# Hybrid encoder layer on one core: the input projection with fp16 high and low parts in place of rounded fp32 parts

## The chip, the cores and the metric

The kernel runs on one core of one Trainium2 chip. The core has five engines with queues of their own: TensorE (PE, matmuls, with its weight loads shown apart as PEld), VectorE (DVE), ScalarE (ACT), GpSimd (POOL) and SyncE (SP, which here only issues DMAs). Each engine works through its queue in order and waits on semaphores of the others. The metric is the device time of one execution in microseconds; lower is better.

## The reference, cut to what matters

One layer of an encoder over x of 2048 tokens and 1024 columns: a norm and an input projection, attention in three dilated windows beside a convolution branch, an output projection, cross-attention to a memory of 256 rows, an MLP, and a last norm. The change is in the first line:

```python
y = rmsnorm(h, norm_mix_g[l]) @ w_in[l]                 # 2048 x 1024 @ 1024 x 2560
q = partial_rotary(y[..., 0:D_ATT]...)                  # 512 columns
k = partial_rotary(y[..., D_ATT:2 * D_ATT]...)          # 512 columns
v = y[..., 2 * D_ATT:3 * D_ATT]...                      # 512 columns
conv = conformer_conv(a, g, ...)                        # 512 columns each; a * sigmoid(g) first
```

All inputs and outputs are float32.

## The kernel before

**Two parts for each operand.** A matmul operand is held as a high part (the value rounded to fp32r, a rounded fp32 format that TensorE reads) and a low part (what the rounding left). `mm3` (L198) makes three matmuls of a product: high by high, high by low, low by high. `wsplit2` (L187) makes the pair of a weight tile of 128 x 1024: ACT copies `raw` to `hi` (L190), DVE or POOL subtracts to `lo` (L191).

**Layout.** x stands transposed: 8 chunks of 128 columns (k) by 4 token groups of 512 (n). `xprep` (L322) loads the natural rows of one group (`xn`), gets the norm's factors per token from squares on ACT (L310), turns each chunk on TensorE (`xt`, L334), stores it for the residual (`xscr`), multiplies by the norm's gain and factor on DVE (`xv`, L339) and splits: ACT to `xh` (L340), POOL to `xl` (L341). A weight tile is 128 output columns of w_in; with 512 tokens it takes 8 x 3 = 24 matmuls (`linear_steps`, into `lin`), moving 512 columns each.

**The units.** `glu` (L507) makes two units for each 128 columns of the convolution branch: g (through a tanh on ACT) and a (times the gate on DVE, stored to `uscr`). `lin_qk` (L606) makes a q or k unit over all four groups; c = "r" gathers the 16 rotary columns of each of the 8 heads with eight DMAs of small pieces, c = 0, 1, 2 the other 48. `lin_v` (L561) makes v with tokens as output rows and 256 columns moving, from weights that were scaled by a power of two per column block (`vscale`, L534: squares of the weights on ACT, a column sum on TensorE, a power on POOL, a bit mask and a reciprocal on DVE). `pinned` and `after` only tell the scheduler that an instruction is to be placed behind another one.

**The order.** `pipeline` (L494) runs the units one after another and keeps two ahead: when unit i starts, the weights of i + 1 are split and the load of i + 2 is issued. A unit's first step issues the DMA of `raw`, its second splits. `raw`, `whi` and `wlo` have two buffers each, so the load of unit i + 2 waits until the low part of unit i is made; the zero row of `edges` (L726) takes a turn in the `raw` buffers between the rotary q tile and the first k tile. All loads stand in SP's queue in a fixed order, so a load that waits holds up those behind it. The units run in this order: g and a of column chunks 0 and 1 for groups 0 and 1; k and q rotary; k and q 0, 1, 2; g and a of chunk 2, v of the first 256 columns, g and a of chunk 3, v of the others; and then, woven into the attention of the first 512 queries, g and a of all four chunks for groups 2 and 3 (`rest`). The projections of the memory for cross-attention (`memory`, L348; their last products are `pb`, evacuated by ACT to `eb`, L464) and the first two groups of x come ahead of all this; groups 2 and 3 of x are prepared while the first units run. The convolution (`conv_unit`, L213, on DVE) runs beside the q, k and v units. The order of each engine's instructions is made by a scheduler from the program's order and its own model of time when the program is built.

## Time and profile before

| | |
|---|---|
| runs, us | 2844.74, 2839.31, 2848.41 |
| median, us | 2844.74 |
| span of the profiled execution, us | 2842.4 |
| DMA | 434.27 MB, mean 153 GB/s |
| projection units ahead of attention | 136.6 to about 524 us (with start and end of `lin` and `v`) |
| late units, woven into attention | about 524 to 713 us |

The profile is of one execution of its own, whose span is the time from its first instruction to its last. Busy times of an engine count its instructions' durations; matmuls are pipelined, so a duration (389 ns for a matmul of 512 columns) is longer than the distance from one start to the next, and it is the latter that says how fast TensorE goes. "Chain" is the work that ended last, followed back from the end. Names are those of the program's tiles: `whi_u<-raw_u` writes `whi_u` from `raw_u`. A row of a group gives its line, engine, operation, names, shape and count, its busy time, and the mean duration in ns. In the timeline the first number is the start from the span's beginning and the second the duration; "[1.69 <-POOL vs L554]" says that the engine was idle for 1.69 us before it, until that instruction ended.

### The profile page before, as it was taken

The numbers are of one execution on the slowest core, as the hardware profiler recorded it, in microseconds if no ns is written. First come the engines' busy times: TensorE is split into PE (matmuls) and PEld (weight loads), VectorE is DVE, ScalarE is ACT, GpSimd is POOL, SyncE is SP. The second block draws the span as 40 slices with busy tenths as digits, with TensorE's granted clock in tenths as the row PEclk, the third lists the DMA queues.
The fourth block names the chain that finished last, engine by engine and source line by source line (L and its number), as shares of the span: only waits on it lengthen the run. The fifth ranks groups of instructions, "written<-read, shape, count | busy, mean of one in ns | idle before, by whom it ended". The sixth has DMA issues, their size and how long they took to land.

```text
span 2842.4 us, 41222 instructions
## 1 busy us (share of the span) xinstructions
PE 2795.1 (98%) x15440; PEld 2355.0 (83%) x15440; DVE 1961.5 (69%) x3473; ACT 1203.8 (42%) x2055; POOL 466.6 (16%) x483
## 2 busy tenths in 40 slices
PE   8999999999999999999999999999999999999998
PEld 7888899888788888888888888888888888888887
DVE  6636536465789786557887755589886646569886
ACT  6633211475554333434443344444433434444443
POOL 1336421122102012200021012001110210000000
PEclk9999999999999999999999999999999999999999
DMA  8979855799734444554444535534444445223332
GB/s 267 304 168 233 203 137 137 182 259 261 201 102 134 128 138 130 166 150 158 122 126 129 149 111 181 176 112 134 130 133 129 142 152 178 90 89 98 92 115 67
DMA packets 590729, 434.27 MB, mean 153 GB/s; under 512 B 191581, under 2 KB 508433, under 8 KB 590016
## 3 DMA queue, kind: packets, MB, share of 16 engines
q1 hardware_dynamic: 549776, 407.68, 50.1%
q10 hardware_dynamic: 38528, 17.93, 2.5%
q0 software_dynamic: 2224, 6.01, 0.6%
q8 instruction: 122, 2.00, 0.3%
q14 instruction: 79, 0.65, 0.1%
HBM read 340.42 MB, written 91.11 MB: 152 GB/s over the span
## 4 chain that ended last, share of the span: by engine, by line
PE 86%; DVE 7%; DMA 3%; issue 1%; ACT 1%; POOL 0%; SPq 0%; DVEq 0%; POOLq 0%; ACTq 0%
PE dn L200 8%; PE dn L201 8%; PE dn L202 8%; PE up L200 7%; PE up L202 7%; PE up L201 7%; PE lin L200 4%; PE lin L202 4%; PE lin L201 4%; PE pt L795 2%; PE o L200 2%; PE o L202 2%; PE o L201 2%; PE xs L200 2%; PE xs L202 2%; PE xs L201 2%
## 5 line engine op out<-in xcount | busy, mean ns | idle before, releaser
L200 PE MATMUL up<-mh,whi_u 128*128 128x512 f32 x1024 | 403.4, 394 | 0.0
L201 PE MATMUL up<-ml,whi_u 128*128 128x512 f32 x1024 | 399.6, 390 | 1.9 <-DVE ml L1239 1.9
L202 PE MATMUL up<-mh,wlo_u 128*128 128x512 f32 x1024 | 399.2, 390 | 0.0
L217 DVE SCALAR_TENSOR_TENSOR cacc<-cu,cw,cacc 128x512 f32<-128x512 f32 x480 | 387.1, 807 | 5.4
L200 PE MATMUL dn<-hhh,whi_d 128*128 128x512 f32 x768 | 299.1, 399 | 1.1 <-ACT hhh L1350 1.1
L201 PE MATMUL dn<-hhl,whi_d 128*128 128x512 f32 x768 | 298.7, 391 | 0.6 <-DVE hhl L1351 0.6
L202 PE MATMUL dn<-hhh,wlo_d 128*128 128x512 f32 x768 | 298.1, 391 | 0.0
L190 ACT CAST whi_u<-raw_u 128x1024 fp32r<-128x1024 f32 x128 | 134.5, 1051 | 262.1 <-PE dn L201 193.3
L190 ACT CAST whi_d<-raw_d 128x1024 fp32r<-128x1024 f32 x100 | 105.1, 1051 | 320.3 <-PE up L201 280.8
L201 PEld LDWEIGHTS up<-ml,whi_u 128*128 128x128 f32 x1024 | 192.5, 188 | 40.6 <-DVE ml L1239 3.2
L202 PEld LDWEIGHTS up<-mh,wlo_u 128*128 128x128 f32 x1024 | 192.2, 188 | 40.5
L200 PEld LDWEIGHTS up<-mh,whi_u 128*128 128x128 f32 x1024 | 192.4, 188 | 37.3
L191 DVE TENSOR_TENSOR wlo_u<-raw_u,whi_u 128x1024 fp32r<-128x1024 f32 x128 | 161.2, 1260 | 40.6 <-ACT whi_u L190 36.1
L1364 DVE TENSOR_TENSOR h<-h,dn 128x512 f32<-128x512 f32 x192 | 128.3, 681 | 84.6 <-PE dn L202 83.7
L1348 DVE SCALAR_TENSOR_TENSOR rl<-up,ssumx 128x512 f32<-128x512 f32 x96 | 65.9, 690 | 172.2 <-PE up L202 171.4
L202 PEld LDWEIGHTS dn<-hhh,wlo_d 128*128 128x128 f32 x768 | 144.1, 188 | 30.7
L200 PEld LDWEIGHTS dn<-hhh,whi_d 128*128 128x128 f32 x768 | 143.7, 188 | 29.7 <-ACT hhh L1350 1.3
L201 PEld LDWEIGHTS dn<-hhl,whi_d 128*128 128x128 f32 x768 | 144.6, 188 | 28.3 <-DVE hhl L1351 1.5
L788 DVE CUSTOM_DVE_ANT_0 sm<-s,mask 128x256 f32<-128x256 f32 (+1 forms) x384 | 127.8, 373 | 58.2 <-PE s L1017 38.9
L177 POOL TENSOR_TENSOR nr<-st_v,mhalf 128x4 f32<-128x4 f32 (+1 forms) x15 | 14.2, 949 | 816.7 <-DVE st_v L173 816.7
L799 DVE TENSOR_TENSOR pl<-pt,ph 128x512 f16<-128x512 f32 x160 | 109.6, 685 | 45.9 <-ACT ph L798 45.6
L789 ACT ACTIVATE sm<-sm,o 128x256 f32<-128x256 f32 (+1 forms) x288 | 116.8, 454 | 55.3 <-DVE o L788 53.9
(459 smaller groups left out, 7060.5 us busy)
## 6 DMA issues: line engine op xcount, KB each, us to landing
raw_u<-in_w_up_dram SPq DMA_DIRECT2D x128, 512.0 KB
raw_d<-in_w_down_dram SPq DMA_DIRECT2D x100, 512.0 KB
raw_o<-in_w_out_dram SPq DMA_DIRECT2D x32, 512.0 KB
raw_a<-ascr SPq DMA_DIRECT2D x32, 512.0 KB
raw_b<-bscr SPq DMA_DIRECT2D x32, 512.0 KB
b<-in_w_down_dram SPq DMA_DIRECT2D x28, 512.0 KB
k<-kscr SPq DMA_DIRECT2D x24, 512.0 KB
k<-kscr SPq DMA_DIRECT2D x8, 1152.0 KB
```

The lines of the kernel that those rows point to most:

```text
L190: ACT.copy(hi, raw)
L191: (lo_eng or DVE).tensor_tensor(lo, raw, f(hi), op=ALU.subtract)
L200: PE.matmul(o, lh, rh, start=first, stop=False, skip_group_check=more)
L201: PE.matmul(o, lh, rl, start=False, stop=False, skip_group_check=more)
L202: last["pe"] = PE.matmul(o, ll, rh, start=False, stop=end, skip_group_check=more)
L217: DVE.scalar_tensor_tensor(acc, u[:, t:t + 512], cw[:, c, t:t + 1], acc, op0=ALU.mult, op1=ALU.add)
L788: last["dve"] = DVE.tensor_tensor_reduce(dst, so, mask[:, 256 * m:256 * m + nk], 1.0, 3e38, ALU.add, ALU.min, mn)
L789: last["act"] = ACT.activation(dst, dst, AF.Exp, bias=mn, scale=-1.0)
L795: last["pe"] = PE.transpose(pt[:, j, :], sm[:, j, :], ident)
L799: DVE.tensor_tensor(pl, pt, ph, op=ALU.subtract)
L1348: last["dve"] = DVE.scalar_tensor_tensor(r, pt, 0.0, rsb, op0=ALU.max, op1=ALU.mult)
L1364: last["dve"] = DVE.tensor_tensor(hs[m], hs[m], pt, op=ALU.add)
```

## The change

x times its gain, and each tile of w_in, are brought to a common magnitude by a power of two and split into two fp16 parts instead of two rounded fp32 parts. The factor for x comes from the norm's gain vector alone (`gmix`), the factor of a weight tile from the sum of its squares: ACT squares the tile and sums along each partition, one matmul by a matrix of ones adds up the partitions and spreads the sum to all of them, POOL takes the power -1/2, DVE multiplies by a target, keeps the exponent bits alone and takes the reciprocal (`pow2`). ACT scales `raw` in place, and then come the copy and the subtraction as before, with fp16 outputs (`wsplit16`). The inverse factors go into what follows: the scale of the tanh for g, the convolution's weights for a, the scales of the q and k evacuations, and for v, whose weights keep their own factors, the evacuation and `vinv`. A tile's factor is found once; the late g and a units use it again. `pipeline` gets one step more for each unit. The code, with what is left out marked:

```diff
...
 VR = 8 * VW
+VT = 4096.0
...
         ACT.activation(cw.rearrange("p a b -> p (a b)"), pv[:, 64:192], AF.Copy, scale=0.5)
+        sq = lp.tile([P, 8], F32, tag="nsq", name="gsq")
+        ACT.activation(sq, gv[:, 0:8], AF.Square, accum_out=sx[:, 3:4])
+        pow2(sx[:, 0:1], sx[:, 1:2], sx[:, 3:4], 1024.0)
+        DVE.tensor_scalar(gmix, gv[:, 0:8], sx[:, 0:1], None, op0=ALU.mult)
+    def pow2(mul, inv, ss, target, *names):
+        with ExitStack() as st:
+            after(st, *names)
+            pc = ps("c", "p2")
+            PE.matmul(pc[:, 0:1], onesq, ss, start=True, stop=True)
+            v = lp.tile([P, 4], F32, tag="p2", name="p2", bufs=2)
+            DVE.tensor_scalar(v[:, 0:1], pc[:, 0:1], 1e-30, None, op0=ALU.max)
+            POOL.tensor_tensor(v[:, 1:2], v[:, 0:1], mhalf, op=ALU.pow)
+            DVE.tensor_scalar(v[:, 2:3], v[:, 1:2], target, None, op0=ALU.mult)
+            DVE.tensor_scalar(mul.bitcast(I32), v[:, 2:3].bitcast(I32), 0x7F800000, None, op0=ALU.bitwise_and)
+            DVE.reciprocal(inv, mul)
+    tiles_scaled = {}
+    def wscale(raw, key):
+        if key in tiles_scaled:
+            return
+        n = tiles_scaled[key] = 4 * len(tiles_scaled)
+        q = lp.tile([P, 1024], BF16, tag="wjunk", name="wjunk")
+        ACT.activation(q, raw.rearrange("p a b -> p (a b)"), AF.Square, accum_out=wsc[:, n + 3:n + 4])
+        pow2(wsc[:, n:n + 1], wsc[:, n + 1:n + 2], wsc[:, n + 3:n + 4], 32768.0, "pe", "dve")
+        t = wsc[:, n + 1:n + 2]
+        DVE.tensor_tensor(t, t, sx[:, 1:2], op=ALU.mult)
+        if key[0] == "a":
+            c = cw[:, key[1]]
+            DVE.tensor_scalar(c, c, t, None, op0=ALU.mult)
+        else:
+            DVE.tensor_scalar(wsc[:, n + 2:n + 3], t, 0.5 if key[0] == "g" else -0.125, None, op0=ALU.mult)
+    def wcol(key, i):
+        n = tiles_scaled[key] + i
+        return wsc[:, n:n + 1]
+    def wsplit16(raw, key, name, lo_eng=None, views=None):
+        hi = wp.tile([P, 8, P], F16, tag="whi", name=f"whi_{name}", bufs=2)
+        lo = wp.tile([P, 8, P], F16, tag="wlo", name=f"wlo_{name}", bufs=2)
+        s = wcol(key, 0)
+        ACT.activation(raw, raw, AF.Copy, scale=s)
+        for of, to in views or ((lambda t: t,) * 2,):
+            ACT.copy(to(hi), of(raw))
+            (lo_eng or DVE).tensor_tensor(to(lo), of(raw), to(hi), op=ALU.subtract)
+        return hi, lo
...
     def gain(key, k):
...
     lp = pool("lin", stack=lin)
+    onesq = lp.tile([P, P], F32, name="onesq")
+    DVE.memset(onesq, 1.0)
+    gmix = lp.tile([P, 8], F32, name="gmix")
+    sx = lp.tile([P, 4], F32, name="sx")
+    wsc = lp.tile([P, 96], F32, name="wsc")
+    lp.tile([P, 248], F32, name="lpad")
...
     def xtiles(n):
...
             for part, dst in (("h", XH_), ("l", XL_)):
-                t = xpool(part, i, n, f"x{part}{i}_{n}")
+                t = xpool(part, i, n, f"x{part}{i}_{n}", dtype=F16)
...
     def load_nat(sp, src, name, bufs=10):
...
             xv = sp.tile([P, 512], F32, tag="xv", name=f"xv{n}_{k}", bufs=2)
-            DVE.scalar_tensor_tensor(xv, pt, gain("mix", k), rbs, op0=ALU.mult, op1=ALU.mult)
+            DVE.scalar_tensor_tensor(xv, pt, gmix[:, k:k + 1], rbs, op0=ALU.mult, op1=ALU.mult)
             ACT.copy(XH_[k, n], xv)
-            POOL.tensor_tensor(XL_[k, n], xv, f(XH_[k, n]), op=ALU.subtract)
+            POOL.tensor_tensor(XL_[k, n], xv, XH_[k, n], op=ALU.subtract)
...
     def t2(name, dtype=F32, shape=(P, 512)):
...
     def pipeline(*units):
 
-        next(units[0])
-        next(units[0])
-        if len(units) > 1:
+        for _ in range(3):
+            next(units[0])
+        for _ in range(2 if len(units) > 1 else 0):
...
                 next(units[i + 2])
-            yield from u
+            for j, _ in enumerate(u):
+                if j == 0 and i + 2 < len(units):
+                    next(units[i + 2])
+                yield
...
     def glu(c, ns, fine=False):
...
             yield
-            wh, wl = wsplit2(wp, raw, f"{x}{c}{ns[0]}", lo_eng=POOL)
+            wscale(raw, (x, c))
+            yield
+            wh, wl = wsplit16(raw, (x, c), f"{x}{c}{ns[0]}", lo_eng=POOL)
...
                     sig[n] = t2(f"sig{c}_{n}")
-                    ACT.activation(sig[n], pt, AF.Tanh, scale=0.5)
+                    ACT.activation(sig[n], pt, AF.Tanh, scale=wcol((x, c), 2))
...
                 dma(sq[q], wcols(w_in, 2 * DATT + P * pr, rows=(4 * q, 4 * q + 4)))
-            for k in range(KC):
-                w = sq[k // 4][:, k % 4]
-                ACT.activation(w, w, AF.Square, scale=gain("mix", k))
+            for q in range(2):
+                w = sq[q].rearrange("p a b -> p (a b)")
+                ACT.activation(w, w, AF.Square)
...
                 POOL.tensor_tensor(v[:, 1:2], v[:, 0:1], mhalf, op=ALU.pow)
-                DVE.tensor_scalar(v[:, 2:3], v[:, 1:2], 512.0, None, op0=ALU.mult)
+                DVE.tensor_scalar(v[:, 2:3], v[:, 1:2], VT, None, op0=ALU.mult)
...
                                   op0=ALU.bitwise_and)
-                DVE.reciprocal(vinv[:, pr:pr + 1], vmul[:, pr:pr + 1])
+                DVE.reciprocal(v[:, 3:4], vmul[:, pr:pr + 1])
+                DVE.scalar_tensor_tensor(vinv[:, pr:pr + 1], v[:, 3:4], VT, sx[:, 1:2], op0=ALU.mult, op1=ALU.mult)
...
     def lin_v(g, ns):
...
         yield
-        wh = lbv.tile([P, 8, 256], F32R, tag="wvh", name=f"wvh{g}{ns[0]}")
-        wl = lbv.tile([P, 8, 256], F32R, tag="wvl", name=f"wvl{g}{ns[0]}")
+        yield
+        wh = lbv.tile([P, 8, 256], F16, tag="wvh", name=f"wvh{g}{ns[0]}")
+        wl = lbv.tile([P, 8, 256], F16, tag="wvl", name=f"wvl{g}{ns[0]}")
...
             ACT.copy(wh[:, :, es], raw)
-            POOL.tensor_tensor(wl[:, :, es], raw, f(wh[:, :, es]), op=ALU.subtract)
+            POOL.tensor_tensor(wl[:, :, es], raw, wh[:, :, es], op=ALU.subtract)
...
             p3 = pt.rearrange("p (h d) -> p h d", d=HD)
-            ACT.copy(st[:, :, 0:HD], p3)
-            last["dve"] = DVE.tensor_tensor(st[:, :, HD + 2:VW], p3, st[:, :, 0:HD], op=ALU.subtract)
+            ACT.activation(st[:, :, 0:HD], p3, AF.Copy, scale=1.0 / VT)
+            last["dve"] = DVE.scalar_tensor_tensor(st[:, :, HD + 2:VW], p3, 1.0 / VT, st[:, :, 0:HD], op0=ALU.mult,
+                                                   op1=ALU.subtract)
...
         nm = f"{'q' if isq else 'k'}{c}"
+        key = ("q" if isq else "k", c)
...
             yield
-            hi = wp.tile([P, 8, P], F32R, tag="whi", name=f"whi_{nm}", bufs=2)
-            lo = wp.tile([P, 8, P], F32R, tag="wlo", name=f"wlo_{nm}", bufs=2)
-            for x in range(2):
-                rv = raw.rearrange("p k (h x j) -> p k h x j", x=2, j=8)[:, :, :, x, :]
-                hv = hi[:, :, x * 64:(x + 1) * 64].rearrange("p k (j h) -> p k h j", h=H)
-                lv = lo[:, :, x * 64:(x + 1) * 64].rearrange("p k (j h) -> p k h j", h=H)
-                ACT.copy(hv, rv)
-                DVE.tensor_tensor(lv, rv, f(hv), op=ALU.subtract)
+            wscale(raw, key)
+            yield
+            views = [(lambda t, x=x: t.rearrange("p k (h x j) -> p k h x j", x=2, j=8)[:, :, :, x, :],
+                      lambda t, x=x: t[:, :, x * 64:(x + 1) * 64].rearrange("p k (j h) -> p k h j", h=H))
+                     for x in range(2)]
+            hi, lo = wsplit16(raw, key, nm, views=views)
...
             yield
-            hi, lo = wsplit2(wp, raw, nm, lo_eng=POOL)
+            wscale(raw, key)
+            yield
+            hi, lo = wsplit16(raw, key, nm, lo_eng=POOL)
...
                 l = lbk.tile([P, 512], F32R, tag="ql", name=f"ql_{nm}{n}", bufs=3)
-                ACT.activation(o, src, AF.Copy, scale=-0.125)
-                last["dve"] = DVE.scalar_tensor_tensor(l, src, -0.125, f(o), op0=ALU.mult, op1=ALU.subtract)
+                ACT.activation(o, src, AF.Copy, scale=wcol(key, 2))
+                last["dve"] = DVE.scalar_tensor_tensor(l, src, wcol(key, 2), f(o), op0=ALU.mult, op1=ALU.subtract)
...
                 s3 = src.rearrange("p (i r) -> p i r", r=16)
-                ACT.copy(fh, s3)
-                last["dve"] = DVE.tensor_tensor(fl, s3, f(fh), op=ALU.subtract)
+                ACT.activation(fh, s3, AF.Copy, scale=wcol(key, 1))
+                last["dve"] = DVE.scalar_tensor_tensor(fl, s3, wcol(key, 1), f(fh), op0=ALU.mult, op1=ALU.subtract)
...
         yield
+        yield
...
```

## The prediction, made before the changed kernel had run

> **What bounds the kernel now.** I read the page first (engines, slices, chain of waits), then stage windows, then the waits of the PE queue in the one part that the change touches, and last the timeline, where the start of each matmul stands.
>
> ```profile
> span 2842.4 us, 41222 instructions
> PE 2795.1 (98%) x15440; PEld 2355.0 (83%) x15440; DVE 1961.5 (69%) x3473; ACT 1203.8 (42%) x2055; POOL 466.6 (16%) x483
> PEclk9999999999999999999999999999999999999999
> PE 86%; DVE 7%; DMA 3%; issue 1%; ACT 1%; POOL 0%; SPq 0%; DVEq 0%; POOLq 0%; ACTq 0%
> ```
>
> TensorE is busy in 98% of the span, carries 86% of the chain that ends last, and its granted clock stays in the top tenth. So a matmul that follows the one before it sooner should pay nearly in full, wherever the stage is TensorE's. Which stages are? The stage windows give, per engine, busy us and (count), then granted clock, DMA share and GB/s. The order is PE, PEld, DVE, ACT, POOL.
>
> ```profile
> 135.00:180.00 45.00, 45.00 (x212) 37.37 (x211) 10.63 (x18) 16.86 (x30) 18.14 (x11) 1.00 0.70 163
> 232.00:300.00 68.00, 68.00 (x305) 56.36 (x305) 48.15 (x56) 21.37 (x37) 42.67 (x38) 1.00 0.94 224
> 390.00:440.00 50.00, 50.00 (x398) 49.09 (x397) 24.28 (x41) 6.90 (x17) 5.24 (x18) 1.00 0.31 86
> 650.00:716.00 66.00, 59.89 (x558) 53.51 (x557) 40.15 (x175) 40.11 (x104) 17.58 (x31) 0.97 1.01 270
> ```
>
> From 135 to some 520 us, where the input projection runs alone, TensorE has no gap; ACT is under half busy there (16.86 of 45, 21.37 of 68) and POOL up to 63% (42.67 of 68). In 650 to 716, where the late gate and value columns are woven into the first attention, TensorE is at 91% and the DMA engines are full (1.01). The waits of the PE queue from 130 to 520 us (us, times, longest) are only two:
>
> ```profile
> PE xt L334 <- DVE xv L339: 1.9, 1, 1.9
> PE pb L200 <- ACT eb L464: 0.7, 1, 0.7
> ```
>
> **The change part by part.** *The matmuls.* x and w_in become fp16 pairs; the three products per chunk stay. They number 4 column chunks x 2 (g, a) x 4 token groups x 8 x 3 = 768, and 8 q/k units x 4 x 24 = 768, all 512 wide, and for v 2 x 16 x 24 = 768 of 256 columns. Of the first 1536, 384 (token groups 2 and 3 of g and a) run late, inside attention. Timeline rows begin with the start in us and the duration:
>
> ```profile
> 284.74 0.39 PE L200 MATMUL lin<-xh,whi_k 128*128 128x512 f32 x1
> ...
> 289.96 0.39 PE L202 MATMUL lin<-xh,wlo_k 128*128 128x512 f32 x1
> 409.80 0.28 PE L202 MATMUL v<-wvh,xl 128*128 128x256 f32 x1
> ...
> 414.96 0.28 PE L200 MATMUL v<-wvh,xh 128*128 128x256 f32 x1
> 590.01 0.19 PE L803 MATMUL opt<-v,ph 128*128 128x65 f16 x1
> ...
> 590.35 0.19 PE L805 MATMUL opt<-v,pl 128*128 128x65 f16 x1
> 590.38 0.47 PE L200 MATMUL lin<-xh,whi_g 128*128 128x512 f32 x1
> 590.69 0.39 PE L201 MATMUL lin<-xl,whi_g 128*128 128x512 f32 x1
> ```
>
> The first pair is the 1st and 24th of a run: 5.22 us / 23 = 227 ns from start to start at 512 columns. The second is the 1st and 44th: 5.16 / 43 = 120 ns at 256. The difference, 107 ns for 256 columns, is 0.418 ns a column, so 13.0 ns of each matmul do not depend on its width. The fp16 run is 12 matmuls of 65, 64 and 65 columns, each with its own weight load: 0.34 / 11 = 30.9 ns, of which 27.0 are columns at the same rate and 3.9 the rest. I carry that 3.9 over to wide fp16 matmuls: 217.9 and 110.9 ns, 9.1 saved each. Nothing in this trace runs fp16 at 512 columns, so the bounds are 0 (the 13 ns belong to any wide matmul) and 13.0. Where TensorE has no gap that is 1152 x 9.1 = 10.5 us and 768 x 9.1 = 7.0.
>
> The Trainium skill, "TensorE: Matmul & The Clock Gate", section "Back-to-back issue gap", gives N/2.4 + 2.5 ns on a warm clock, 215.8 at 512 columns; by that estimate the saving of all 2304 matmuls would be some 25.5 us instead of the 21 that 9.1 gives. The fp32 rows at 227 and 120 do not follow that formula.
>
> *The late 384.* At 9.1 they are worth 3.5 us. The last two timeline rows add something: the first wide matmul after a short fp16 run takes 0.31 us to the next start, 0.08 more than 227 ns, because a weight load of 188 ns does not fit under a 31 ns matmul; an fp16 load takes 97.
>
> ```profile
> L200 PEld LDWEIGHTS lin<-xh,whi_g 128*128 128x128 f32 x128 | 24.2, 189 | 3.2
> L803 PEld LDWEIGHTS <-ph 128*128 128x128 f16 x640 | 60.1, 97 | 9.3 <-issue 7.2 <-ACT rl L1349 0.5 <-ACT ph L798 0.4
> ```
>
> That could be 128 groups of three x 0.08 = 10 us more, in a stage whose DMA engines are full. I take 5 of the 13.7 (bounds 0 and 13.7). Sum of the gains: 10.5 + 7.0 + 5 = 22.5.
>
> *Passes over the weights.* Each of 16 weight tiles gets a Square with a sum (1.05 us), each of 24 loads a scaling in place before the old copy (1.05), v none; the eight 128x128 squares of each v column block become two of 512. ACT gets 17 instructions more (40 passes x 1.05 = 42 us over 580, less what the merged squares save), DVE 106 tiny ones (0.15 each, 16 us), POOL 17 powers (0.55 each).
>
> ```profile
> L190 ACT CAST whi_g<-raw_g x8: 1040/1052/1055, 133.8 to 614.0; 128x1024 fp32r<-128x1024 f32 x8
> L191 POOL TENSOR_TENSOR wlo_g<-raw_g,whi_g x8: 2375/2394/2410, 134.9 to 615.2; 128x1024 fp32r<-128x1024 f32 x8
> ```
>
> A q or k unit lasts 96 x 0.227 = 21.8 us, so two more ACT passes (2.1) and a POOL subtraction with fp16 on two sides, which this trace lacks (between half and double the 2.39), lie under it. I cost them at nothing there; were POOL three times slower, the low part would still come 15 us ahead.
>
> *Column sums on TensorE.* Seventeen new fp32 matmuls of one column stand in the PE queue, each waiting for a Square. Their shape is that of the v scales:
>
> ```profile
> 349.85 0.50 PE L551 MATMUL vss<-ones,vsq 128*128 128x1 f32 x4
> 350.21 0.49 PE L200 MATMUL lin<-xh,whi_q 128*128 128x512 f32 x1
> 350.54 0.40 PE L201 MATMUL lin<-xl,whi_q 128*128 128x512 f32 x1
> 351.36 0.15 DVE L553 TENSOR_SCALAR vs<-vss 128x1 f32<-128x1 f32 x1
> 352.61 0.55 POOL L554 TENSOR_TENSOR vs<-vs,mhalf 128x1 f32<-128x1 f32 x1
> 353.20 0.15 DVE L555 TENSOR_SCALAR vs<-vs 128x1 f32<-128x1 f32 x1 [1.69 <-POOL vs L554]
> ```
>
> Four cost 0.36, and the wide one behind them 0.33 instead of 0.23: 0.15 for a single one, 17 x 0.15 = 2.5 us. DVE's next step waits behind POOL (1.69 here); what queues on DVE is evacuations and convolution, and with five accumulator banks of 5.4 us each that is covered.
>
> *The start.* Here nothing covers the longer path. Today the first tile is copied and subtracted while the last memory matmuls run, with its first products mixed in among them:
>
> ```profile
> 122.77 0.48 SPq L57 DMA_DIRECT2D raw_g<-in_w_in_dram  x1
> 133.81 1.05 ACT L190 CAST whi_g<-raw_g 128x1024 fp32r<-128x1024 f32 x1
> 134.94 2.40 POOL L191 TENSOR_TENSOR wlo_g<-raw_g,whi_g 128x1024 fp32r<-128x1024 f32 x1
> 136.62 0.48 PE L200 MATMUL lin<-xh,whi_g 128*128 128x512 f32 x1
> ```
>
> In the changed program's order the column sums of the first two tiles stand behind the last memory matmul, and ACT scales both tiles before it copies the first. From that matmul on: sum and scale 1.7 (0.25 + 0.15 + 0.55 + 0.15 + 0.15 and hand-overs; 3.7 by the v rows, where DVE and POOL were occupied), three ACT passes 3.2, POOL's low part 2.4, together 7.3, less eight products that go ahead (1.7): 5.6, taken as 6, bounds 4 and 10.
>
> *The tiles of q/k rotary columns and the first k tile.* Two raw buffers serve all tiles, and SP issues in order. After the change the loads of the last x group (tokens 1536 on) all stand behind the rotary loads on SP, and those wait for the low parts of g and a, which come later.
>
> ```profile
> 154.38 3.77 SPq L57 DMA_DIRECT2D raw_kr<-in_w_in_dram  x6
> 165.26 3.67 SPq L57 DMA_DIRECT2D raw_qr<-in_w_in_dram  x6
> 181.53 1.36 SPq L57 DMA_DIRECT2D vtok<-zrow  x2
> 189.57 2.29 SPq L57 DMA_DIRECT2D raw_k<-in_w_in_dram  x3
> 392.81 1.05 ACT L190 CAST whi_a<-raw_a 128x1024 fp32r<-128x1024 f32 x1 [5.40 <-DMA raw_a<-in_w_in_dram]
> 388.81 0.38 SPq L57 DMA_DIRECT2D raw_a<-in_w_in_dram  x1
> ```
>
> The first k tile shares its buffer with the zero row: 8.0 us from that store to the load's issue, 2.3 of issuing, 4.0 to land (388.81 to 392.81), 1.3 for the Square: 15.6 after the rotary tile is done with. Its column sum stands only 24 products (5.2 us) into the rotary unit. Today that tile has a lead of some 5 us, so up to 15.6 - 5.2 - 5 = 5.4 us are waited for, and the x transposes queued behind wait too. I take 5 for this whole stretch (bounds 0 and 15, three such waits). Later sums stand where their load has had a unit's time.
>
> Sum: -22.5 + 2.5 + 6 + 5 = -9. The profiled execution has a span of 2842.4; the sum gives 2833.4. The runs' median is 2844.74 (2839.31 to 2848.41), 2.3 above that span, so about 2835 for a median.
>
> **The rivals** (times for a median, 2.3 over the span). *Full gain*: waits hide as they do today, and late loads pay: -30 + 2.5 + 4, some 2821. For it: only 2.6 us of PE waits from 130 to 520. Against: the start has no cover. *Given back*: the stretch around the rotary tiles costs its 15 us; -22.5 + 2.5 + 6 + 14 = 0, about 2845. For it: SP blocked behind the raw buffers. *Slower, by the queued column sums*: each stands in an in-order queue before products that need nothing of it; if the weights' landings are late against the planned order, TensorE stops at each. It decides from 0.9 us a sum on ((22.5 - 2.5 - 6) / 16 = 0.9); at 1.6 it gives 26 us, some 2857. For it: DMA share 0.94 in the q/k stage. Against: a load is issued a whole unit ahead. *The change doesn't shorten wide matmuls*: a 188 ns load is hidden under 227 anyway; then 7 + 2 are gained against 13.5, some 2849. Against: 13 against 3.9 ns.
>
> This last is what the Trainium skill says in "TensorE: Matmul & The Clock Gate", section "Weight-path perf modes", of fast weight load: that it pays at small free dimensions. The weight-load rows, 97 against 188, agree that fp16 loads are faster; no row shows what that does at 512.
>
> **How the numbers follow.** Forecast 0.48, full gain 0.13, given back 0.19, slower by sums 0.13, wide not shortened 0.07. A measurement of this kernel can tell about 0.3%, 8.5 us. Of the forecast's own spread (2824 to 2842) some two thirds lie under 2836: faster 0.32 + 0.13 = 0.45; same 0.16 + 0.19 + 0.05 = 0.40; slower 0.13 + 0.02 = 0.15. The range, 2816 to 2856, takes in full gain and most of the slow case.
>
> **What would show it.** Products at 216 to 218 ns start to start, v at 109 to 111; a TensorE gap of 5 to 7 us between the last memory matmul and the first full run of products; gaps ahead of the column sum of the first k tile, small ones elsewhere; the same work from 760 us on, shifted only. Wrong: the period stays at 227, or gaps stand ahead of most sums.

## The result: slower by 36 us, and the profile after

| | before | changed |
|---|---|---|
| median of four runs, us | 2844.44 | 2880.28 |
| range, us | 2839.31 to 2848.41 | 2877.83 to 2885.74 |
| ratio, 95% interval | | 1.013 (1.0113 to 1.0147) |
| span of the profiled execution, us | 2842.4 | 2876.2 |

The forecast was 2835, range 2816 to 2856. The page of the changed kernel:

```profile
span 2876.2 us, 41437 instructions
PE 2783.7 (97%) x15474; PEld 2211.0 (77%) x15474; DVE 1979.6 (69%) x3579; ACT 1250.5 (43%) x2089; POOL 467.2 (16%) x500
```

TensorE is busy for 11.4 us less than before (2795.1) in a span that is 33.8 us longer: the matmuls did get shorter, and what came instead is idle time. The timeline shows the shorter matmuls, the 1st and 24th of a q/k run and the 1st and 44th of a v run, as in the prediction:

```profile
342.76 0.38 PE L251 MATMUL lin<-xl,whi_q 128*128 128x512 f16 x1
...
347.72 0.38 PE L250 MATMUL lin<-xh,whi_k 128*128 128x512 f16 x1
424.62 0.27 PE L250 MATMUL v<-wvh,xh 128*128 128x256 f16 x1
...
429.31 0.27 PE L251 MATMUL v<-wvl,xh 128*128 128x256 f16 x1
```

4.96 / 23 = 216 ns and 4.69 / 43 = 109 ns, 11 ns less each. The stage windows (busy us and count of PE, PEld, DVE, ACT, POOL, then granted clock, DMA share, GB/s), the first four those of the prediction:

```profile
135.00:180.00 45.00, 40.97 (x202) 22.16 (x201) 13.51 (x41) 23.40 (x37) 17.97 (x15) 0.96 0.57 135
232.00:300.00 68.00, 66.31 (x317) 30.91 (x316) 48.49 (x74) 29.99 (x40) 48.41 (x44) 1.00 0.96 228
390.00:440.00 50.00, 49.81 (x384) 37.43 (x383) 20.05 (x42) 14.12 (x24) 12.52 (x25) 1.00 0.47 127
650.00:716.00 66.00, 58.32 (x563) 45.98 (x560) 37.64 (x164) 39.40 (x101) 12.81 (x20) 0.95 0.96 245
...
140.00:200.00 60.00, 51.17 (x244) 25.63 (x245) 24.64 (x57) 31.65 (x47) 21.64 (x18) 0.94 0.53 125
530.00:720.00 190.00, 166.41 (x1523) 130.18 (x1522) 108.97 (x454) 116.80 (x278) 40.03 (x51) 0.94 0.84 220
```

Two stretches went wrong. In the first, from 140 to 200 us, TensorE had no gap before and now stands for 8.8 of 60 us; it goes on beyond 200 us, for from 200 to 320 us TensorE stands for 10.4 of 120 us (1.9 before), and only from 232 us on is the early stage nearly gapless again. The second is the late units. The mean granted clock fell to 0.94 in both windows as well (1.00 and 0.97 before). The waits of PE from 130 to 520 us, which were two before, name the first:

```profile
PE p L173 <- ACT wjunk L189: 8.0, 3, 5.4
PE lin L250 <- ACT whi_g L209: 3.8, 1, 3.8
PE rb L235 <- DVE rsx L230: 3.2, 1, 3.2
PE xt L390 <- DMA xn<-in_x_dram: 2.3, 1, 2.3
```

These are column sums (p) that wait for a Square, the first tile's high part, and the preparation of x. The longest, 5.37 us up to 210.53 us, is the column sum of the first k tile, whose Square has waited 9.80 us on ACT for the tile's load. The start, row by row of the timeline (start, duration, engine; in brackets the wait and who ended it):

```profile
139.12 0.38 PE L173 MATMUL p<-wsc,onesq 128*128 128x1 f32 x2 [0.25 <-DVE p L175]
140.11 1.15 ACT L207 ACTIVATE raw_g<-raw_g,wsc 128x1024 f32<-128x1024 f32 x1 [0.58 <-DVE wsc L178]
142.20 1.03 ACT L209 CAST whi_g<-raw_g 128x1024 f16<-128x1024 f32 x1
143.29 0.61 PE L250 MATMUL lin<-xh,whi_g 128*128 128x512 f16 x1 [3.78 <-ACT whi_g L209]
143.69 0.63 PE L251 MATMUL lin<-xl,whi_g 128*128 128x512 f16 x1
144.11 0.63 PE L250 MATMUL lin<-xh,whi_g 128*128 128x512 f16 x1
```

TensorE waits 3.78 us, and the products behind the wait start 0.40 to 0.43 us apart instead of 0.216: the granted clock is 0.50 from 144 to 146 us and 1.00 again from 147 us on. This agrees with the Trainium skill, "TensorE: Matmul & The Clock Gate", section "What's actually happening", which says that an idle window of about 3.4 us is enough to halve the clock until a busy one has passed. The 426.7 ns that the same page gives for 512 columns at half clock, in its section "Wait — 56ns, not 53.3ns?", are close to the 0.40 to 0.43 us seen here. So a wait of some 4 us costs more than its length, which no term of my sum had.

On SP's queue the loads of x (xn) and of the rotary tiles stand like this:

```profile
145.46 0.37 SPq L58 DMA_DIRECT2D raw_g<-in_w_in_dram  x1
...
159.66 4.98 SPq L58 DMA_DIRECT2D raw_kr<-in_w_in_dram  x7
...
165.84 0.65 SPq L58 DMA_DIRECT2D xn<-in_x_dram  x1
...
174.97 5.24 SPq L58 DMA_DIRECT2D raw_qr<-in_w_in_dram  x8
```

The third weight tile is loaded at 145.46 (137 us before), the first rotary one at 159.66 (154.38), the second at 174.97 (165.26), since each waits for the low part of an earlier tile.

The late units, in the timeline around 545 us, and ACT's waits from 520 to 760 us:

```profile
540.55 0.38 SPq L58 DMA_DIRECT2D raw_a<-in_w_in_dram  x1
545.24 1.15 ACT L207 ACTIVATE raw_a<-raw_a,wsc 128x1024 f32<-128x1024 f32 x1 [5.75 <-DMA raw_a<-in_w_in_dram]
546.30 1.26 ACT L854 ACTIVATE sm<-sm,o 128x128 f32<-128x128 f32 x4
546.73 1.35 PE L860 MATMUL pt<-ident,sm 128*128 128x128 f32 x4 [4.90 <-ACT sm L854]
```
```profile
ACT raw_g L207 <- DMA raw_g<-in_w_in_dram: 14.1, 2, 12.4
ACT raw_a L207 <- DMA raw_a<-in_w_in_dram: 11.0, 2, 5.7
```

ACT's queue reaches the scaling of a weight tile 5.75 us before the tile is in memory. Behind it in the same queue stand attention's exponentials (sm), and TensorE waits 4.90 us for them. TensorE's waits for exponentials from 520 to 760 us, now and before, and ACT's longest wait at a late weight tile before:

```profile
PE pt L860 <- ACT sm L854: 12.6, 4, 5.4
PE pt L795 <- ACT sm L789: 3.6, 1, 3.6
ACT whi_a L190 <- PE lin L201: 9.3, 1, 9.3
```

Before, the first instruction on a weight tile was the copy into `whi`, which waits for TensorE to be done with that buffer (the last row); no wait of ACT for the load of one of these tiles stands in that view of before. The scaling in place needs no buffer, so it waits for the load.

Last, the loads of the output projection's operands (cath, catl) and TensorE's waits for them:

```profile
724.90 1.75 SPq L58 DMA_DIRECT2D cath<-cath  x2
733.18 0.32 SPq L58 DMA_DIRECT2D uscr<-u  x1
736.95 0.50 SPq L58 DMA_DIRECT2D catl<-catl  x1
743.92 1.25 SPq L58 DMA_DIRECT2D catl<-catl  x2
750.59 0.79 PE L251 MATMUL o<-catl,whi_o 128*128 128x512 f32 x1 [6.20 <-DMA catl<-catl]
```

and before:

```profile
695.88 0.81 SPq L57 DMA_DIRECT2D cath<-cath  x2
...
704.90 1.56 SPq L57 DMA_DIRECT2D catl<-catl  x2
...
714.02 0.33 SPq L57 DMA_DIRECT2D uscr<-u  x1
```

Before, twelve of these loads stood ahead of the last store of a late unit (uscr, 714.02); now only two do, and the output projection stops for the others.

### The profile page after: what moved, and what is told of

It is laid out like the page before. It is cut to its first block, busy times and chain, and to the rows that moved or that the text cites. A ratio compares the mean times of both kernels' runs of the same rounds, so it can differ in the third digit from the quotient of the medians.

```text
span 2876.2 us, 41437 instructions
## 1 busy us (share of the span) xinstructions
PE 2783.7 (97%) x15474; PEld 2211.0 (77%) x15474; DVE 1979.6 (69%) x3579; ACT 1250.5 (43%) x2089; POOL 467.2 (16%) x500
## 4 chain that ended last, share of the span: by engine, by line
PE 59%; DVE 5%; DMA 2%; ACT 1%; issue 1%; POOL 1%; SPq 0%; ACTq 0%; POOLq 0%; DVEq 0%
PE dn L250 7%; PE dn L252 7%; PE dn L251 7%; PE up L250 7%; PE up L252 7%; PE up L251 7%; DVE cacc L267 2%; PE o L251 2%; PE o L250 2%; PE o L252 2%; PE xs L250 2%; PE xs L252 2%; PE xs L251 1%; PE s L1082 1%; DMA cath<-lh 1%; PE pt L860 1%
## 5 line engine op out<-in xcount | busy, mean ns | idle before, releaser
L227 POOL TENSOR_TENSOR nr<-st_v,mhalf 128x4 f32<-128x4 f32 (+1 forms) x15 | 14.3, 950 | 817.3 <-DVE st_v L223 817.3
```

## The experiments

The table goes with all of them. Each ratio is to the kernel before on the same chip. A lag is the start of one and the same matmul (the k-th of its name) in the run's timeline, less its start in the profile of before: at the first g unit (145 us), in the rotary q unit (217), in the first g unit of the late ones, which still runs ahead of attention (507), at the end of the late ones (714), and in the output projection (757). So each stretch has its own account. From 757 us on nothing is changed, and lags stay within 3 us of their value there but for e3 (20.8) and e8 (5.0).

A lag compares two single executions. The changed kernel, e4 and e5 have the same instructions in the same order on TensorE up to 467 us, and their lags still differ by up to 3.8 us at 145 (5.6 and 9.4) and 3.5 at 217 (18.9 and 22.4). At 507 the changed kernel and e5 lie 0.5 apart; at 714, with the order on TensorE still the same, 4.5. A difference of that size in a column is not shown to be an edit's. Where two builds take the three products of a chunk in another order, the choice of the matmul also moves an entry of the first two columns by up to some 1.3 us.

| run | median, us | ratio (95% interval) | 145 | 217 | 507 | 714 | 757 |
|---|---|---|---|---|---|---|---|
| changed | 2880.28 | 1.013 (1.0113 to 1.0147) | 5.6 | 18.9 | 8.7 | 19.1 | 31.3 |
| e1 | 2880.64 | 1.0115 (1.0093 to 1.0137) | 8.2 | 23.4 | 16.9 | 32.2 | 32.5 |
| e2 | 2823.81 | 0.9922 (0.9907 to 0.9937) | -1.1 | -1.7 | -20.0 | -23.9 | -23.6 |
| e3 | 2899.93 | 1.0185 (1.0167 to 1.0203) | 5.2 | 15.7 | 19.8 | 36.5 | 36.7 |
| e4 | 2880.37 | 1.0118 (1.0096 to 1.0139) | 9.4 | 21.8 | 14.4 | 21.3 | 34.3 |
| e5 | 2867.82 | 1.0072 (1.0053 to 1.0091) | 7.5 | 22.4 | 8.2 | 23.6 | 22.5 |
| e6 | 2854.41 | 1.0032 (1.0019 to 1.0045) | 5.2 | 10.6 | -7.3 | 8.1 | 8.5 |
| e7 | 2838.81 | 0.9977 (0.9964 to 0.999) | -0.3 | 7.4 | -8.3 | -7.8 | -7.1 |
| e8 | 2876.63 | 1.0111 (1.0096 to 1.0126) | 5.7 | 13.4 | 15.9 | 26.3 | 26.4 |
| e9 | 2875.26 | 1.0103 (1.0084 to 1.0122) | 7.5 | 18.1 | 14.0 | 26.3 | 26.9 |
| e10 | 2863.02 | 1.0054 (1.0037 to 1.007) | 10.0 | 22.6 | 10.7 | 17.5 | 17.9 |
| e11 | 2882.15 | 1.0121 (1.0106 to 1.0136) | 14.4 | 26.5 | 32.6 | 35.4 | 35.9 |
| e12 | 2839.66 | 0.9974 (0.9964 to 0.9984) | 1.3 | 1.0 | -17.4 | -20.9 | -9.6 |
| e13 | 2862.3 | 1.0061 (1.0038 to 1.0085) | 5.5 | 15.3 | 3.1 | 19.5 | 19.8 |
| e14 | 2873.45 | 1.0099 (1.0084 to 1.0115) | -1.3 | 11.9 | 9.6 | 25.8 | 26.1 |
| e15 | 2857.86 | 1.0042 (1.0029 to 1.0056) | 7.7 | 19.9 | 8.2 | 12.7 | 11.5 |
| e16 | 2847.28 | 1.0007 (0.9998 to 1.0016) | -3.3 | 11.7 | -1.6 | -0.2 | 0.1 |
| e17 | 2841.61 | 0.9986 (0.9977 to 0.9996) | -1.8 | 1.3 | -11.0 | -8.7 | -7.7 |
| e18 | 2845.09 | 0.9998 (0.9988 to 1.0008) | -1.8 | 2.3 | -5.9 | -4.9 | -4.7 |

### fp16 alone, and the chain alone (e2, e3, e8)

e2 splits the weights without a factor, so that they are no longer brought to a common magnitude, and x alone keeps its factor:

```diff
-        s = wcol(key, 0)
-        ACT.activation(raw, raw, AF.Copy, scale=s)
```

> fp16 parts alone: weights are split without any factor (no Square, no column sum, no power, no scaling in place; x keeps the factor from the gain, and its inverse stands as a constant column in what follows), memory as in e1. Theory (the chain of sums and scaling costs, not fp16): 2304 matmuls x 11 to 11.5 us per thousand = 26 us less than before, some 2818. Rival (fp16 operands themselves cost, through the clock or through shorter cover for every load): 2840 or more.

2823.81, 23.4 us less than the before of the same chip (2847.25). fp16 does what it was forecast to do; lags fall to -20.0 by 507 us and to -23.9 by 714. Only between 145 and 217 us does it gain 0.6 where 287 matmuls at 11 ns each would be some 3: there TensorE waits 3.1 us for xv and 1.1 for rsx (before, 1.9 for xv and none for rsx), so some of the cover is gone with fp16 alone.

e3 keeps squares, sums, powers and the scaling, and leaves all parts in rounded fp32 (a filler at the top of memory had to be cut by 320 bytes to make room):

```diff
-        hi = wp.tile([P, 8, P], F16, tag="whi", ...
+        hi = wp.tile([P, 8, P], F32R, tag="whi", ...
```

> The chain alone: squares, column sums, powers and the scaling in place as in the changed kernel, but all parts of x and w_in stay rounded fp32, and the memory of x is that of before. Theory: what the changed kernel lost is the chain's: 28 us up to the late units and 16 in them, 44 in all, some 2888. Rival (the chain is only late because fp16 makes each unit shorter): under half of that, 2865 or less.

2899.93, but 21 us of that were lost after 757 us, where no instruction differs, evenly: the lag there grows from 36.7 to 57.5 at 2808 us. So e8 leaves the filler out whole, a shift by 1024 bytes:

> e3 with the filler at the top of memory left out whole (1024 bytes) instead of cut by 320 bytes. In e3 fp32 matmuls took 229 to 231 ns from start to start where their moving operand lay on the shifted side, 227 elsewhere, and 21 us were lost after 760 us where nothing is changed. Theory (a shift of 320 bytes, not the chain): 227 again everywhere, some 2878. Rival (the chain or the chip of that run): 2895 to 2900 and 230 ns again.

2876.63. Two runs of 24 dn matmuls, the first of e3, the second of e8:

```profile
1261.76 0.40 PE L250 MATMUL dn<-hhh,whi_d 128*128 128x512 f32 x1
...
1267.13 0.39 PE L252 MATMUL dn<-hhh,wlo_d 128*128 128x512 f32 x1
```
```profile
1245.73 0.39 PE L250 MATMUL dn<-hhl,whi_d 128*128 128x512 f32 x1
...
1250.95 0.39 PE L249 MATMUL dn<-hhh,whi_d 128*128 128x512 f32 x1
```

5.37 / 23 = 233 ns against 5.22 / 23 = 227. Of e3's 53 us some 21 are thus a matter of where the tiles lie. In e8 the lag by 757 us is 26.4: 15.9 up to 507, 10.4 in the late units. That is the chain and, besides, the Square's junk output in a shared scratch tile, which e3 and e8 have in common with e1 below; what that tile costs with fp32 parts was not tried. With fp16 the chain costs more: e5 below, with group 2's space as in e2, lags e2 by 28.2 us at 507 (8.2 + 20.0) and loses 19.3 more by 714 (23.6 - 8.2 + 23.9 - 20.0). That the shorter units leave less cover is an explanation for the difference that fits the gap in e2, and was not tried by itself.

### The halves of the chain (e6, e7)

e6 scales by a constant, with no square, sum or power; e7 finds the factors and does not use them (each is multiplied by its inverse):

> fp16 parts with a constant factor 2048: ACT still scales each tile in place before the copy, but no Square, no column sum, no power; memory as in e2. Theory (the sums cost the early part, the scaling the late one): up to 520 us as e2, then some 8 to 10 us lost between 520 and 720 us by ACT's queue standing on the weight DMA: e2 + 9, some 2833. Rival (nearly all is the sums'): 2824.

> Squares, column sums and powers stay, but the weights are split without the scaling in place (the found factor is multiplied by its inverse); memory as in e5. Theory: the whole early loss of the chain (28 us up to the late units) and none in the late stage: e2 + 28, some 2852. Rival (the scaling pass costs as much as the sums, early too): 2840 or less.

The scaling, thought the smaller half, is the larger: e6 comes to 2854.41 instead of 2833, e7 to 2838.81 instead of 2852. In e6 5.4 of its lag stand already before the first weight tile is used (a pb product at 136 us), 4.8 of them at 100 us, ahead of any scaling, so they are not the scaling's; 15.4 come between 507 and 714 us. e7 loses 0.5 there. ACT's waits from 520 to 720 us in e6:

```profile
ACT raw_g L201 <- DMA raw_g<-in_w_in_dram: 17.6, 2, 13.8
ACT raw_a L201 <- DMA raw_a<-in_w_in_dram: 14.0, 2, 8.0
```

No sum is left in this kernel, and the same wait stands there. Early, e7 loses 11.7 to e2 by 507 us and e6 7.3 beside its 5.4; the 28.2 of both together (e5) are more than their sum. In e7 no weight waits for a factor and in e6 the factor is always there, which would explain it; no run tests that by itself.

### The memory (e1, e5, e12)

Before, the 32 KB of the output projection's operands for one token group lay over the x tiles of group 2 alone. With smaller x tiles the last of them lies, by the sizes of the tiles (no trace shows addresses), over a tile of group 3 too, which is in use for longer. e1 gives group 2 its old space:

```diff
-                t = xpool(part, i, n, f"x{part}{i}_{n}", dtype=F16)
-                dst[2 * i, n], dst[2 * i + 1, n] = t[:, 0], t[:, 1]
+                t = xpool(part, i, n, f"x{part}{i}_{n}", (P, 2, 1024 if n == 2 else 512), F16)
+                dst[2 * i, n], dst[2 * i + 1, n] = t[:, 0, 0:512], t[:, 1, 0:512]
```

> The changed kernel with the memory of before: each x tile of token group 2 keeps the space that it had (1024 fp16 columns of which 512 are used), the junk output of the Square goes into a shared scratch tile, two fillers are shorter; no arithmetic changes. Theory (layout): the loads of the output projection's operands (cath, catl) lie over group 2 alone again, stand ahead of the last uscr store in SP's queue, and the 12 us lost from 738 to 754 us come back: some 2868, no long waits of o on catl. Rival (the loads are late because everything before them is late): the same time as the changed kernel, 2880.

No gain in the total. The table says why: from 714 to 757 us e1 loses 0.3 where the changed kernel loses 12.2, so the layout is the cause of that loss; but it came there 13 us later. The edit had also put the Square's junk output into a shared tile; e5 gives it one of its own:

> e1 again, but the Square's junk output keeps a tile of its own (as uint8, 1 KB), so that it no longer waits for the shared scratch tiles; fillers of 1 KB and 0.7 KB are left out. Theory: e1 took the 12 us back at 738 us and lost 8 to 14 earlier through the shared tile; here early and late stages go as in the changed kernel and the 12 us stay: 2868. Rival (the 12 us are refunded whatever comes before, or the early loss belongs to the layout): 2876 to 2882.

2867.82, as expected; it reaches 714 us with 8.6 us less lag than e1, so most of those 13 went with the shared tile (two fillers are left out as well). The other 4.5 are the difference between the changed kernel and e5 with the same order on TensorE, for which no run has a cause. SP's queue in e5:

```profile
718.67 1.16 SPq L58 DMA_DIRECT2D cath<-cath  x2
...
728.36 1.01 SPq L58 DMA_DIRECT2D catl<-catl  x2
...
737.68 0.33 SPq L58 DMA_DIRECT2D uscr<-u  x1
```

The loads are ahead of the last store again. e12 shows the loss without the chain, fp16 alone in the changed kernel's memory:

> e2 (no factors for the weights) with the memory that the changed kernel has (x tiles of group 2 half the size, fillers as in the changed kernel). Theory (smaller x tiles alone put the output projection's operands over group 3, which is free later): the 12 us at 719 to 754 us are lost without any chain: 2824 + 12 = 2836. Rival (it needs the late stage to be late as well): 2824.

2839.66, and 11.3 of it between 714 and 757 us. So these 12 us come with fp16's smaller tiles, not with the chain.

### The late units (e4, e10, e15)

e4 has POOL scale the eight late tiles in place:

> The changed kernel, but the eight late tiles (groups 2 and 3 of g and a) are scaled in place by POOL instead of ACT. Theory: ACT's queue no longer stands on the weight DMA with the exponentials of attention behind it; the waits of pt on sm from 520 to 720 us fall from 12.6 us to some 4, and with them the half-clock stretches: 2866 to 2870. Rival (the late loss comes from the fuller DMA or from the later start): 2880.

Not as expected: 2880.37. ACT's waits on weight DMAs are gone and the step at 533 to 545 us too (lags 13.0 and 14.6; the changed kernel 7.4 and 15.1), and from 507 to 714 us it loses 6.9 instead of 10.4. But at 507 it was 5.7 us behind the changed kernel already. Its timeline shows where most of that arose: 1.2 us at 465 us, 5.9 at 475. POOL's queue stands 4.24 us on the load of the first late tile (raw_g), scales it at 469.48 for 2.85 us, and only then, at 472.31, makes a low part of v's weights that the changed kernel made at 467.75; TensorE waits 2.19 us for it, and the granted clock over 474 to 478 us is 0.57. It is the same fault on another engine: the first reader of a load, with work that is due queued behind it. The total hid both the gain and the loss.

e10 folds the factor into the copy, for all tiles, so that ACT's first touch waits for the buffer of `whi` as before; POOL scales `raw` behind it (2.85 us each in e4):

```diff
-        ACT.activation(raw, raw, AF.Copy, scale=s)
-        ...
-            ACT.copy(to(hi), of(raw))
+            ACT.activation(to(hi), of(raw), AF.Copy, scale=s)
+        POOL.tensor_scalar(raw, raw, s, None, op0=ALU.mult)
```

> e5, but ACT no longer scales in place: it writes the high part as scale x raw in one pass, which waits for the buffer of the high part as in the kernel before; POOL then scales raw in place and subtracts. Theory (ACT's queue standing on the weight DMA ahead of attention's exponentials costs 14 to 18 us between 520 and 720 us): 2868 - 15 - some 4 earlier = 2849, ACT waits for no DMA of a weight there. Rival (any engine that waits for the late weights costs the same, as with e4): 2865.

2863.02, not the 2849 expected: 8.6 us fewer lost late (6.8 instead of 15.4), 2.5 more lost at the start, where POOL's pass is on the way to the first low part; those 2.5 are no more than the spread of that column. e15 does it for the late tiles alone:

> e5, but for the eight late tiles alone ACT writes the high part as scale x raw in one pass and POOL scales raw afterwards. Theory: the 15 us lost in e5 between 520 and 720 us fall to 5 to 8, as in e10: 2868 - 8 = 2860; no wait of ACT for a weight DMA there. Rival: 2868.

2857.86, and 4.5 us lost late instead of the 15.4 of e5 (10.4 in the changed kernel). Its order on TensorE is e5's up to 672 us. Its waits of ACT from 520 to 760 us have the row of the kernel before back, a wait for the buffer:

```profile
ACT whi_a L211 <- PE lin L256: 8.6, 1, 8.6
```

### The early units (e9, e11, e13, e14, e16 to e18)

e9 puts square and sum where the split stands, one unit later; e11 adds e10's fold:

> e5, but a tile's square and column sum stand where its split stands, at the start of the unit before its own, instead of one step after its load was issued. Theory (the early loss is the sums standing in TensorE's queue before their load has landed, 8 us between 164 and 205 us alone): e5's 2868 falls to some 2856, and p no longer waits around the rotary tiles. Rival (the chain is now right ahead of the copy and the low parts come too late for the g and a units of 10 us): 2868 or more.

> e9 and e10 together: factors found on the chip, fp16 parts, memory of before. Theory: e2 (fp16 alone, ratio 0.992) plus the start's 6 us and 2.5 us of column sums: 2832 to 2836, faster than before. Rival (costs of both kinds remain): 2845 or more.

Both wrong: 2875.26 and 2882.15. What e9 won at the rotary k tile was lost again by q and k tiles whose high part came late; in e11, with POOL's pass in the same chain, the lag at 507 is 32.6. The place of the sums alone isn't the cause. e13 gives x's natural rows 16 buffers, so that no load of x stands behind a weight load that waits; e14 lets the first two column sums stand among the memory's products:

```diff
-    def load_nat(sp, src, name, bufs=10):
+    def load_nat(sp, src, name, bufs=16):
```
```diff
-..., 32768.0, "pe", "dve")
+..., 32768.0, *(("pe", "dve") if n > 4 else ()))
```

> e5 with 16 buffers instead of 10 for the natural rows of x, so that in SP's queue the loads of x of group 3 stand ahead of all weight loads instead of behind those that wait for low parts. Theory (of the 12 to 15 us lost between 172 and 200 us most is x prepared late): some 10 us come back, 2868 to 2858, and no xt waits for xn, no rb for rsx. Rival (the chain on ACT and POOL itself is late there): 2865 to 2868.

> e5, but the first two column sums are no longer bound behind the last memory product and stand among the memory products. Theory: the first tile's factor is there some 5 us earlier; the 8 us lost between the last pb and the first lin fall to 1 or 2, and the next loads, which wait for that tile's low part, move with it: 2868 - 7 = 2861 or less. Rival (what is won at the start is waited for at the rotary tiles): 2866 to 2868.

e13 wins 5.1 us by 507 (3.1 against 8.2), half of what was expected, and 2862.3 in all (2856.8 to 2873.4). e14, at 2873.45 slower than e5 and than either side of its expectation, takes the whole start back (-1.3 against 7.5 at 145) and is 10.5 ahead of e5 at 217, but gives it all back by 507. Its waits of PE from 125 to 500 us:

```profile
PE p L172 <- ACT wjunk L188: 9.0, 3, 5.2
PE p L172 <- DVE vs L612: 5.7, 1, 5.7
```

Column sums again: TensorE came earlier to sums that were not ready. e16 joins e13, e14 and e15:

> e13, e14 and e15 together. Theory (the three are separate losses): 2868 - 10 - 7 - 8 = 2843, level with before; rival (they are one delay seen in three places): 2855 or more.

2847.28, level with before. What is left at 170 to 200 us shows in e16's timeline:

```profile
177.62 1.06 ACT L188 ACTIVATE wjunk<-raw_qr 128x1024 uint8<-128x1024 f32 x1 [4.50 <-DMA raw_qr<-in_w_in_dram]
...
180.18 4.70 ACT L211 ACTIVATE whi_kr<-raw_kr 128x512 f16<-128x512 f32 x2
182.68 4.69 DVE L215 TENSOR_TENSOR wlo_kr<-raw_kr,whi_kr 128x512 f16<-128x512 f32 x2 [7.82 <-ACT whi_kr L211]
```

The late units' fault in small: ACT's queue stands 4.50 us on the Square of the next tile, whose load has not landed, and behind it wait the copy of the tile that is due and, behind the subtraction that needs that copy, DVE's whole queue with the evacuations of x. e17 binds each Square behind the copy of the tile before it:

```diff
+        with ExitStack() as st:
+            after(st, "whi")
             ACT.activation(q, ..., AF.Square, accum_out=wsc[:, n + 3:n + 4])
...
+            last["whi"] = ACT.activation(to(hi), of(raw), AF.Copy, ...)
```

> e16 with each Square bound behind the high-part copy of the tile before it in ACT's queue. Theory (a Square that waits for its load holds the copy and the casts behind it): the 12 us lost between 175 and 200 us in e16 fall to 4 or 5; 2847 - 8 = 2839, faster than before. Rival (the copy is late by the chain itself, or a later Square makes its own tile late): 2845 or more.

2841.61, a ratio of 0.9986 with an interval that just excludes 1, and the lag at 217 falls from 11.7 to 1.3. In its timeline the copy comes first and the Square no longer waits:

```profile
173.41 4.75 ACT L213 ACTIVATE whi_kr<-raw_kr 128x512 f16<-128x512 f32 x2
177.67 1.34 ACT L190 ACTIVATE wjunk<-raw_qr 128x1024 uint8<-128x1024 f32 x1
```

> e17, and the factor of a tile two units ahead is found after the third token group of a q or k unit instead of after the first. Theory: no sum of a q or k tile waits any more; e16 shows 2 to 3 us of such waits from 200 to 420 us, so some 2837. Rival: the same as e17 within 2 us.

2845.09, against 2837 expected: it loses 5.1 us to e17 by 507 us. Sums of q and k tiles that stand later are no gain.

## Why the prediction was wrong

The account at 757 us, from e2's and the changed kernel's rows of the table: fp16 -23.6; the chain up to 507 us 28.7 (8.7 + 20.0); the chain in the late units 14.3 (19.1 - 8.7, and the 3.9 that e2 gains there); the memory 11.9 (12.2, less 0.3 in e2). Together 31.3, the lag that was measured; the terms are differences of rows, so that they add up proves nothing by itself. The gain, the late units and the memory are each tried by taking them out (e2, e15, and e1 with e5 and e12).

- **The gain** was right in sum: 22.5 forecast, 23.4 in e2's median. Two terms were off and nearly cancel: 11 ns a matmul instead of 9.1, and 3.9 us between 507 and 714 us in e2, which is the 384 late matmuls at 11 ns (4.2), so nothing is seen of what was added for late weight loads. The formula of the page "TensorE: Matmul & The Clock Gate" of the Trainium skill, section "Back-to-back issue gap", had the time of a matmul closest: 215.8 at 512 columns, 216 measured; the same section says that the formula is too long for a stream of loads and matmuls, with some 131 ns at 512 columns, and the 216 here contradict that.
- **The start**, 6 (bounds 4 and 10), was right: 6.7 behind e2 at 145 us (8.6 in e5), gone in e14.
- **The rotary stretch** was mis-sized: taken at 5 of 0 to 15, it cost 13.9 ((18.9 - 5.6) against (-1.7 + 1.1) in e2). The wait at the column sum of the first k tile was forecast at up to 5.4 and was 5.4. Left out was what stands behind a waiting instruction on ACT: the Square of one tile ahead of the copy of another and of the casts of x (e16, e17), and the half clock after long gaps.
- **"Later sums stand where their load has had a unit's time"** failed: from 217 to 507 us the changed kernel gained 10.2 us where e2 gained 18.3. Its sums are queued one token group after the load's issue, not a unit, as I had read for the first k tile and then not applied to the others. From 236 us on TensorE waits 4.3 us for such sums, about half of the 8.1 that are missing. That a later place would save them is not shown: e18 placed sums later and lost.
- **"I cost them at nothing there"**, of the passes over the weights, is the step that failed outright. The cover that I named, a unit of 21.8 us, is that of the q and k units. In the late units ACT serves attention, TensorE waits for ACT's exponentials, and the scaling in place was a new first reader of a load with no buffer to wait for: 14.3 us there. e15 is e5 with the late tiles scaled in another way, and that takes back 10.9 of the 15.4 us that e5 loses from 507 to 714 us; without any scaling the loss there is 0.5 (e7). Nor do the passes lie wholly under the early units: with no sum at all, e6 loses 7.3 us to e2 by 507 us beside the 5.4 of its start.
- **The memory** was in no term. That tiles of half the size move what lies over them, and so the point at which later loads may start, cost 11.9 us (e12, e5).
- **The rival "slower, by the queued column sums"** had the right kind of mechanism, an in-order queue that stands on a load, on the wrong engine: sums with unused factors cost 15 us in all (medians of e7 and e2), the scaling alone 31, some 5 of them ahead of the first tile and not its own (e6).

The half clock can be bounded from the granted clock: 0.94 over the 60 us from 140 us and 0.96 over the 120 us from 200 us, both 1.00 before, are at most 3.6 + 4.8 = 8.4 of the chain's early 28.7 us. From 530 to 720 us, 0.94 instead of 0.97 is at most 5.7. These are upper bounds, since a clock at half costs nothing while TensorE waits anyway.

Of the 17 to 18 us that remain between e17 and e2 the table places 15.9: 3.0 up to 217, 6.0 from there to 507, 6.2 in the late units, and 0.7 up to 757. What causes them stays open, and so does why the chain costs more with fp16 than with rounded fp32 parts.

The fastest version is e2, 0.9922 of before, if the weights need no factor of their own; with factors found on the chip it is e17, 0.9986.

## What to carry to other kernels

Ask of every new instruction that reads a loaded tile what made its predecessor wait: if it was a buffer and is now the load, the whole queue of that engine will stand on the load, and busy times do not show it. When a tile changes size, look up what later shares its memory. And judge an edit by the lag of the same matmul stretch by stretch, since a total can hide a gain (e1) as well as a loss (e4), but learn first how far two executions of the same code lie apart.

## What the runs showed of the hardware

A gap of 3.8 us on TensorE is followed by matmuls of 512 columns 400 to 430 ns apart, at a granted clock of 0.50, for some 3.4 us (an estimate from 0.61, 0.50, 0.50 and 0.68 in the four stretches of 1 us from 143 us on, in the changed kernel).

fp16 operands shorten a matmul that follows its predecessor at once by 11 ns, at 512 columns (227 to 216 ns) and at 256 (120 to 109).

A shift of 320 bytes of the tiles on one side of memory made rounded fp32 matmuls of 512 columns take up to 233 ns instead of 227 from start to start, at a granted clock of 1.00, and added 20.8 us to the lag after 757 us (e3). With a shift of 1024 bytes the distance was 227 ns again and the lag grew by 5.0 us (e8). The fillers that this kernel holds are not idle.
